# Values from unnormalised, host-transposed rows; forgetting heads first; their output projection moved into attention

## The chip, the core and the metric

The kernel runs on one core of one Trainium2 chip. The metric is the device time of one execution in microseconds (us), here the median of the runs of one kernel. The engines are named as in the profile: PE does matmuls (PEld is its weight load), DVE and ACT do elementwise work and read the banks that PE writes, POOL does slower elementwise work, and SP issues every DMA of this kernel, in the order of the program.

## What is computed

One layer on x of 1024 rows by 1024 columns, in float32. The part that the change touches, from the reference:

```python
h = rmsnorm(x, g_mix_pre)
fq, fk, fv, f_logit, cq, ck, cv = split(h @ w_in)          # 8 + 8 heads of 64
y_fox = forgetting_attention(fq, fk, fv, f_logit + b_fgt)  # causal; logits + c[t] - c[s]
                                                           # with c = cumsum(log_sigmoid(f_logit))
y_chk = chunked_relpos_attention(cq, ck, cv, rel_bias)     # own chunk of 64 + 8 before, relative bias
y = concat(rmsnorm(y_fox, g_fox_out), rmsnorm(y_chk, g_chk_out))
x = x + rmsnorm(y @ w_out, g_mix_post)
```

Cross-attention into 256 memory rows and a squared-ReLU MLP of width 4096 follow; of them the change touches only where the keys and values of the memory stand in the order of the work.

rmsnorm divides a row by the root of its mean square and multiplies it by a gain per column. A row's factor can therefore be applied after a product with weights, while the gain per column must go in ahead of it.

## The kernel before, in words

**Products.** Every product is in split form: each operand is a high part, rounded to the fast matmul type, plus a low part, the rest. mm3 (L191 to L195) issues three matmuls per product: high by high, low by high, high by low. A high part is an ACT copy out of a bank or a load (L187, L231, L404), its low part a DVE or POOL subtraction (L188, L232, L406 to L413).

**Banks.** The eight banks go in pairs under the tags mm, s, tr and pv. A pair under mm serves the projections: a third product waits until the evictions have emptied the first.

**Start-up (L1345 to L1404)**, written out by hand. Rows of x come in 128 at a time (L266); ACT squares and sums them (L208), POOL takes the root (L202, L203), DVE multiplies by root and gain (L272), PE transposes them 128 by 128 (L218), ACT and DVE split the result into hT, high and low (L231, L232). A gain row is spread over the partitions by two matmuls with ones (gpre, L1356). Behind each two blocks of rows the values of half of the heads are projected (values, L306 to L322): v1, the chunked heads' first half, and v0, the forgetting heads' first half with the eight gate columns (264 columns). The relative-bias rows are loaded, turned round and stored to DRAM between them (bias_rows, L280 to L286: rsrc, rrow, rd), and the first three weight blocks of the stock are loaded and two of them split.

**Attention phase (L1333)**. From here Flow (L58 to L135) writes out the order: streams of PE steps, each with a planned cost and a condition; work for DVE, ACT, POOL and DMA issue (V, S, G, D) is put into a planned time line and emitted in its order. The streams, by priority: value_steps (L686: pv, the products of probabilities and values), turn_steps (L649: transposes of probabilities), score_steps (L559), side_steps (L809: forget gates, then transposes of later values), rstd_steps(0) and, as filler, filler_steps (L1322): projections of q, k and from pair 4 also v for each pair of heads, then memory keys and values. Pairs go in ORDER (L325): chunked 0 and 1, forgetting 0 to 3, chunked 2 and 3. Stock (L346) loads weight blocks ahead into three buffers and splits them; Biases (L512) loads the row bias or the cumulative gate (cd) of each head; Outputs (L941) reloads the finished heads.

The forget gates (L469 to L493) are eight small transposes, a chain of ten DVE steps and three ACT steps with two table loads over 8 rows of 1024, which ends in a scan (L492) and a store to cd (L493).

**pv (L686 to L716).** A step covers two key blocks by two query blocks, of which one corner can be masked off ("dead"). The dead quarter of ph and pl, the split probabilities, is set to zero on POOL (L665, L666), and the step has four matmuls of 256 columns (L708, L709). When a unit is done, ACT copies 64 partitions of the bank (L715), DVE adds the other 64 (L716), and one DMA stores the result to od.

**Second phase.** filler: mix_steps(0) and mix_steps(1) (L1085), the two halves of the output projection, the second added to the first; then the memory queries and so on to the MLP.

Of the kernel before, what the change touches and what calls it, by code (L numbers as in the profile page):

```python
# [14 lines left out]
F32 = mybir.dt.float32  # L15
# [120 lines left out]
def build(ctx, tc, nc, out, t):  # L136
# [16 lines left out]
    def u4(name, shape, dt=F32R):  # L153

        return up.tile(list(shape), dt, tag="u4", bufs=30, name=name)
# [16 lines left out]
    wcount = [0]  # L172

    def load_w(src, shape, alloc=None, lo_on=None):
        n = wcount[0]
        wcount[0] += 1
        raw = wp.tile(shape, F32, tag="wraw", bufs=3, name=f"wraw{n}")
        nc.sync.dma_start(raw, src)
        return split_w(raw, shape, n, alloc, lo_on)

    def split_w(raw, shape, n, alloc=None, lo_on=None):
        if alloc is None:
            hi = wp.tile(shape, F32R, tag="whi", bufs=2, name=f"whi{n}")
            lo = wp.tile(shape, F32R, tag="wlo", bufs=2, name=f"wlo{n}")
        else:
            hi, lo = alloc(f"whi{n}", shape), alloc(f"wlo{n}", shape)
        nc.scalar.activation(hi, raw, AF.Copy)  # L187
        (lo_on or nc.gpsimd).tensor_sub(lo, raw, f(hi))  # L188
        return hi, lo

# [15 lines left out]
    def rms(x, scratch, name):  # L206
        ss = small.tile([P, 1], F32, tag="ss", bufs=8, name=f"ss_{name}")
        nc.scalar.activation(scratch, x, AF.Square, scale=1.0 / 32.0, accum_out=ss)  # L208
        return rstd_of(ss, f"rstd_{name}")

    def to_T(xa, xb, act, c0, name, tags=("tr", "tr")):

        trs = [mm_tile([P, 2, 2, P], f"tr_{name}_{k}", tags[k // 4]) for k in range(0, KC, 2)]

        def turn(k, q):
            xn = (xa, xb)[q]
            for j in range(2):
                nc.tensor.transpose(trs[k // 2][:, j, q, :], xn[:, (k + j) * P:(k + j + 1) * P], ident)  # L218

        ahead = tags[0] != tags[1]  # L220
        if ahead:
            for k in range(0, KC, 2):
                turn(k, 0)
        for k in range(0, KC, 2):
            if not ahead:
                turn(k, 0)
            turn(k, 1)
            src = trs[k // 2].rearrange("p a q b -> p a (q b)")
            i, o = k // act.per, k % act.per
            dh = act.h[i][:, o:o + 2, c0:c0 + 256]  # L230
            nc.scalar.activation(dh, src, AF.Copy)  # L231
            nc.vector.tensor_sub(act.l[i][:, o:o + 2, c0:c0 + 256], src, f(dh))  # L232


# [6 lines left out]
    ones = const.tile([1, P], F32, name="ones")  # L241
# [4 lines left out]
    od = [[dr.tile([P, HT], F32, name=f"od{k}_{h}") for h in range(2)] for k in range(KC)]  # L246
# [15 lines left out]
    hT = [Act(f"hT{h}") for h in range(2)]  # L262
    def load_x(b):
        tag = "sp" if b % 3 else "klo"
        xt = p1.tile([P, D], F32, tag=tag, bufs=5 if b % 3 else 4, name=f"x_{b}")
        nc.sync.dma_start(xt, t["x"][b * P:(b + 1) * P, :])  # L266
        return xt

    def norm_x(xt, b):
        junk = p1.tile([P, D], BF16, tag="ph", bufs=2, name=f"junk{b}")  # L270
        r = rms(xt, junk, f"x{b}")
        nc.vector.scalar_tensor_tensor(xt, xt, r, gpre, op0=ALU.mult, op1=ALU.mult)  # L272

# [14 lines left out]
    fcol = p1.tile([P, TB, 8], F32, tag="o2", bufs=2, name="fcol")  # L288

    def value_weights(g, raws=None, only=None):  # L290

        n = 264 if g == 0 else 256
        src = t["w_v0"] if g == 0 else t["w_v1"]
        raws = [] if raws is None else raws
        for i, (a, b) in enumerate(((0, 3), (3, 6), (6, 8)) if g == 0 else ((0, 4), (4, 8))):
            if only in (None, i):
                raw = wp.tile([P, b - a, n], F32, tag="wraw", bufs=3, name=f"wrawv{g}{a}")
                nc.sync.dma_start(raw, src[:, a:b, :])
                raws.append(raw)
        return raws  # L300

    def value_split(g, raw, i, lo_on=None):
        k = raw.shape[1]
        wh, wl = split_w(raw, list(raw.shape), f"v{g}{i}", None if g == 1 else u4, lo_on)
        return [(wh[:, j, :], wl[:, j, :]) for j in range(k)]

    def value_tiles(g):

        return [u4(f"vs{g}_{i}", (P, 2, 4, P)) for i in range(4)]

    def values(g, w, vs, kb):
        act, cs = hT[kb // 4], slice((kb % 4) * P, (kb % 4 + 1) * P)
        n = 264 if g == 0 else 256
        ps = mm_tile([P, n], f"v{g}_{kb}")
        for kc in range(KC):
            mm3(ps, act.hi(kc, cs), act.lo(kc, cs), *w[kc], kc == 0, kc == KC - 1)
        src = ps[:, 0:256].rearrange("p (h d) -> p h d", d=64)
        dh = vs[kb // 2][:, kb % 2, :, 0:64]
        nc.scalar.activation(dh, src, AF.Copy)
        if g == 0:  # L320
            nc.scalar.activation(fcol[:, kb, :], ps[:, 256:264], AF.Copy)
        nc.vector.tensor_sub(vs[kb // 2][:, kb % 2, :, 64:128], src, f(dh))  # L322


    ORDER = (("c", 0), ("c", 1), ("f", 0), ("f", 1), ("f", 2), ("f", 3), ("c", 2), ("c", 3))  # L325
# [3 lines left out]
            dict(s=2, tr=2, pv=2, mm=2, sp=1, p=2, klo=4, bias=2, raw=2, w=0, u4=6,  # L329
# [16 lines left out]
    class Stock:  # L346
# [3 lines left out]
        def __init__(self):  # L350
            self.blocks = []
            for n, (kind, pr) in enumerate(ORDER):
# [9 lines left out]
            self.blocks += [(("mk", nb), t["w_mk"][nb], [P, KC, P]) for nb in range(KC)]  # L362
            self.blocks += [(("mv", nh, kp), row_pair(t["w_mv"], kp, nh), [P, 2, HT])
                            for nh in range(2) for kp in range(4)]
            pair = [P, 2, HT]
            self.blocks += [(("wo", g, nh, i), row_pair(t["w_out"], 2 * g + i, nh), pair)
                            for g in range(2) for nh in range(2) for i in range(2)]
# [5 lines left out]
            self.home = {("wo", 0, 1, 0): "wq", ("wo", 0, 1, 1): "u4", ("wo", 1, 1, 0): "wq", ("wo", 1, 1, 1): "u4"}  # L373
# [95 lines left out]
    def forget_gates():  # L469

        z, e, l, u = [p1.tile([8, S], F32, tag="sp", bufs=5, name=f"f{n}") for n in "zelu"]
        parts = []
        for g in range(2):
            tr = mm_tile([8, 4, P], f"ftr{g}", "tr")
            for j in range(4):
                nc.tensor.transpose(tr[:, j, :], fcol[:, g * 4 + j, :], ident)
            parts.append(("V", 0.75, lambda g=g, tr=tr: nc.vector.tensor_scalar(
                z[:, g * HT:(g + 1) * HT], tr.rearrange("p a b -> p (a b)"), bfgt, None, op0=ALU.add)))
# [16 lines left out]
        def done(at):  # L495
            seen["gates"] = at
            for _ in range(4):
                free["sp"].give(at)

        for _ in range(2):  # L500
            free["tr"].take()
        flow.chain(flow.end, parts[:2], lambda at: [free["tr"].give(at) for _ in range(2)] and
                   flow.chain(at, parts[2:], done))


# [53 lines left out]
    def score_steps():  # L559
# [5 lines left out]
        for n, a in heads:  # L565
            kind, pr = ORDER[n]
            h = pr * 2 + a
            for g in groups(n):
                probs[n, a, g] = {}
                for q in (1, 0) if kind == "f" else (0, 1):  # L570
# [9 lines left out]
                    for j, (o, w) in enumerate(pieces):  # L580
# [21 lines left out]
                        if not last:  # L602
                            flow.put("V", flow.end, 0.15 + w / 950, reduce, free["s"].give)
                        else:
# [17 lines left out]
                            go = lambda at, w=w, reduce=reduce, after=after: flow.put("V", at, 0.15 + w / 950, reduce, after)  # L622
# [26 lines left out]
    def turn_steps():  # L649
        for n, a, g in units:  # L650
            for c, (kbs, slots, dead) in enumerate(key_steps(n, g)):
# [6 lines left out]
                whole = all_of(("t", n, a, g, c), 1 + len(dead))  # L658
# [3 lines left out]
                for m, (j, q) in enumerate(slots):  # L662
                    if m in dead:
                        def zero(ph=ph, pl=pl, m=m):
                            nc.gpsimd.memset(f(ph[:, m, :]), 0.0)  # L665
                            nc.gpsimd.memset(f(pl[:, m, :]), 0.0)  # L666
                        flow.put("G", flow.now, 0.45, zero, whole)
                    else:
                        sp, b0, i = probs[n, a, g][q]
                        k = kbs[j] - b0  # L670
                        nc.tensor.transpose(tr[:, m, :], sp[:, k * P:(k + 1) * P], ident)  # L671

                def split(at, ph=ph, pl=pl, tr=tr, live=live, whole=whole):
# [3 lines left out]
                    flow.put("V", at, 0.7, lambda: nc.vector.tensor_sub(pl[:, live, :], tr[:, live, :],  # L677
                                                                        f(ph[:, live, :])), done)

                flow.put("S", flow.end, 0.6, lambda ph=ph, tr=tr, live=live: nc.scalar.activation(  # L680
# [5 lines left out]
    def value_steps():  # L686
        landed = [all_of(("od", k), 32) for k in range(2)]
        for n, a, g in units:
            kind, pr = ORDER[n]
            h = pr * 2 + a  # L690
            own, oth = HALVES[a]
            kcol = pr if kind == "f" else 4 + pr
            steps = key_steps(n, g)
            for c, (kbs, slots, dead) in enumerate(steps):
                yield (0.48, lambda: there(("t", n, a, g, c), ("v", n, 0), ("v", n, 1))
                       and (c or free["pv"].ready()))
# [4 lines left out]
                for half in range(2):  # L701
                    kb = kbs[slots[2 * half][0]]
                    if n < 4:
                        v = vs[0 if kind == "f" else 1][kb // 2][:, kb % 2, (pr % 2) * 2 + a, :]
# [1358 lines left out]
```

## Time and profile before

| | us |
|---|---|
| median of 3 runs | 1495.92 (1494.37 to 1496.46) |
| the profiled execution: its time and its span | 1496.46, 1496.5 |
| PE busy, share of the span | 1475.1, 99% |
| DVE, ACT, POOL busy | 938.1, 789.8, 403.4 |
| first value matmul; first matmul of q | 11.96; 65.54 |
| end of the gates' scan | 91.55 |

How to read the rows below. A row of the table of windows is a stretch (start and end in us, its length), then for PE, PEld, DVE, ACT and POOL busy time and number of instructions, then the granted clock of PE (1.00 is full), the mean busy share of the DMA engines, and GB/s. A row of the timeline is start, length, engine, line, operation, output<-inputs, tile shapes and count, and in brackets the engine's idle time just before it with what ended that. A group row is line, engine, operation and shape, xcount, then busy us, mean ns of one, then idle time ahead of the group and what ended most of it. A DMA row has count, KB each, and us from issue to landing.

### The profile page before, as it was taken

The numbers are of one execution on the slowest core, as the hardware profiler recorded it, in microseconds if no ns is written. First come the engines' busy times: TensorE is split into PE (matmuls) and PEld (weight loads), VectorE is DVE, ScalarE is ACT, GpSimd is POOL, SyncE is SP. The second block draws the span as 40 slices with busy tenths as digits, with TensorE's granted clock in tenths as the row PEclk, the third lists the DMA queues.
The fourth block names the chain that finished last, engine by engine and source line by source line (L and its number), as shares of the span: only waits on it lengthen the run. The fifth ranks groups of instructions, "written<-read, shape, count | busy, mean of one in ns | idle before, by whom it ended". The sixth has DMA issues, their size and how long they took to land. (4 is left out here: it accounts for less than half of the span.)

```text
span 1496.5 us, 21618 instructions
## 1 busy us (share of the span) xinstructions
PE 1475.1 (99%) x7628; PEld 1254.1 (84%) x7628; DVE 938.1 (63%) x1617; ACT 789.8 (53%) x1405; POOL 403.4 (27%) x629
## 2 busy tenths in 40 slices
PE   8999999999999999999999999999999999999998
PEld 7989888888889888888888887888888888888886
DVE  6377677565576834884375577775555675646577
ACT  5367576575666835554354455555555553444442
POOL 4244355353354300521031423333333000000021
PEclk9999999999999999999999999999999999999999
DMA  4223312512225552461241355774445685436465
GB/s 170 90 74 89 84 44 88 152 55 65 73 66 149 173 177 85 137 213 59 85 169 57 112 183 186 265 246 147 150 150 176 234 340 202 140 120 215 173 252 197
DMA packets 82766, 218.58 MB, mean 146 GB/s; under 512 B 9801, under 2 KB 13905, under 8 KB 82658
## 3 DMA queue, kind: packets, MB, share of 16 engines
q1 hardware_dynamic: 82658, 217.20, 43.5%
q8 instruction: 60, 0.98, 0.3%
q14 instruction: 48, 0.39, 0.1%
HBM read 157.86 MB, written 50.91 MB: 140 GB/s over the span
## 5 line engine op out<-in xcount | busy, mean ns | idle before, releaser
L677 DVE TENSOR_TENSOR pl<-ptr,ph 128x512 fp32r<-128x512 f32 (+1 forms) x152 | 92.2, 616 | 39.7 <-ACT ph L680 33.7
L1789 ACT ACTIVATE whif<-ra 128x1024 fp32r<-128x1024 f32 x37 | 39.2, 1060 | 122.2 <-PE fy L194 62.6
L1791 DVE TENSOR_TENSOR wlof<-ra,whif 128x1024 fp32r<-128x1024 f32 x37 | 45.3, 1225 | 91.0 <-ACT whif L1789 91.0
L680 ACT ACTIVATE ph<-ptr 128x512 fp32r<-128x512 f32 (+1 forms) x152 | 79.3, 540 | 39.0 <-PE ptr L671 32.4
L1905 POOL TENSOR_SCALAR rf<-sf 128x1 f32<-128x1 f32 x8 | 8.2, 1026 | 326.4 <-ACT jf L1890 326.1
L709 PE MATMUL pv<-pl,vs 128*128 128x256 f32 x304 | 78.9, 283 | 2.6 <-DVE pl L677 2.6
L708 PE MATMUL pv<-ph,vs 128*128 128x256 f32 x304 | 79.8, 286 | 0.0
L194 PE MATMUL fx<-vlof,whif 128*128 128x512 f32 x168 | 65.4, 389 | 0.0
L193 PE MATMUL fx<-vhif,whif 128*128 128x512 f32 x168 | 65.4, 389 | 0.0
L195 PE MATMUL fx<-vhif,wlof 128*128 128x512 f32 x168 | 65.4, 389 | 0.0
L709 PEld LDWEIGHTS pv<-pl,vs 128*128 128x128 f32 x304 | 57.6, 189 | 7.4 <-DVE pl L677 2.2
L708 PEld LDWEIGHTS pv<-ph,vs 128*128 128x128 f32 x304 | 57.3, 188 | 4.0
L1679 POOL TENSOR_TENSOR sc<-wf,wf 128x512 f32<-128x512 f32 x14 | 21.3, 1524 | 142.3 <-DMA wf<-in_w_ff 95.4
L193 PE MATMUL k<-hT_hi,whik 128*128 128x512 f32 x128 | 52.7, 412 | 0.0
L193 PE MATMUL mq<-h2T_hi,whimq 128*128 128x512 f32 x128 | 51.6, 403 | 0.0
L193 PE MATMUL q<-hT_hi,whiq 128*128 128x512 f32 x128 | 50.9, 398 | 0.0
L193 PE MATMUL ym<-whimo,oT_hi 128*128 128x512 f32 x128 | 50.3, 394 | 0.1
L194 PE MATMUL yw<-wlowo,yT_hi 128*128 128x512 f32 x128 | 49.9, 390 | 0.3 <-DVE wlowo L410 0.3
L195 PE MATMUL k<-hT_hi,wlok 128*128 128x512 f32 x128 | 50.2, 392 | 0.0
L194 PE MATMUL mq<-h2T_lo,whimq 128*128 128x512 f32 x128 | 50.1, 391 | 0.1
L193 PE MATMUL yw<-whiwo,yT_hi 128*128 128x512 f32 x128 | 50.1, 392 | 0.0
L194 PE MATMUL k<-hT_lo,whik 128*128 128x512 f32 x128 | 50.1, 391 | 0.0
(596 smaller groups left out, 5029.2 us busy)
## 6 DMA issues: line engine op xcount, KB each, us to landing
ra<-gd SPq DMA_DIRECT2D x56, 512.0 KB, 3.9
wg<-in_w_ff SPq DMA_DIRECT2D x56, 512.0 KB, 6.0
wf<-in_w_ff SPq DMA_DIRECT2D x38, 512.0 KB, 4.0
gd<-s SPq DMA_DIRECT2D x48, 256.0 KB, 2.1
wrawmq<-in_w_mq SPq DMA_DIRECT2D x16, 512.0 KB, 3.8
wrawmo<-in_w_mo SPq DMA_DIRECT2D x16, 512.0 KB, 3.8
gd<-u SPq DMA_DIRECT2D x32, 256.0 KB, 2.1
gd<-g SPq DMA_DIRECT2D x25, 256.0 KB, 2.5
```

The lines of the kernel that those rows point to most:

```text
L193: nc.tensor.matmul(ps, lh, rh, start=start, stop=False, skip_group_check=more)
L194: nc.tensor.matmul(ps, lh, rl, start=False, stop=False, skip_group_check=more)
L195: nc.tensor.matmul(ps, ll, rh, start=False, stop=stop, skip_group_check=more)
L677: flow.put("V", at, 0.7, lambda: nc.vector.tensor_sub(pl[:, live, :], tr[:, live, :], f(ph[:, live, :])), done)
L680: flow.put("S", flow.end, 0.6, lambda ph=ph, tr=tr, live=live: nc.scalar.activation(ph[:, live, :], tr[:, live, :], AF.Copy), split)
L708: nc.tensor.matmul(pv, v, ph[:, hs, :], start=c == 0 and half == 0, stop=False)
L709: nc.tensor.matmul(pv, v, pl[:, hs, :], start=False, stop=c + 1 == len(steps) and half == 1)
L1679: eng.tensor_sub(sc[:, k1], r0[:, k0], r1[:, k0])
L1789: nc.scalar.activation(ah, ra, AF.Copy)
L1791: nc.vector.tensor_sub(al, ra, f(ah))
L1905: nc.gpsimd.tensor_scalar(r, ssf[b][:, 0:1], ssf[b][:, 1:2], EPS, op0=ALU.add, op1=ALU.add)
```

## The change

1. **Start-up.** x also comes transposed from the host (x_t, 128 columns of x by 512 rows per piece). Its pieces are multiplied by the gain and split (plain_split), with no root yet. The values are projected from them, and a row's root goes in when they leave the banks (values_out). Squares are still summed from rows of x; the root, on POOL, is set on four diagonals, and a matmul with ones spreads it over the partitions (spread). DVE then normalises x_t in place (norm) and it is split again into hT for q and k (norm_split). The 64 transposes of x and the gpre matmuls are gone. Values first projected are now both halves of the forgetting heads; the chunked values come with the pairs.
2. **Order.** Forgetting pairs 0 to 3, then chunked 0 to 3. The forget gates move from side_steps into the start-up, between norm and norm_split of the second half; both parts of bias_rows come after them. The first pair is projected as q and k of the first 512 columns, then q and k of the second.
3. **pv.** No zeros are written; a matmul on a half with a dead quarter has 128 columns instead of 256 (160 of 608).
4. **Leaving the pv bank.** One ACT copy of 128 by 256 and two stores, high and low half apart; Outputs loads both (16 more loads of 256 KB) and adds them, on POOL for the forgetting heads, on DVE for the chunked.
5. **mix_steps(0)** goes into attention's filler, after the memory keys and ahead of the memory values. Its result is stored to yd and loaded again for mix_steps(1) (Back).
6. **Planner.** Planned costs of three steps are lower (reduce, ph, pl), 34 buffers of the kind u4 instead of 30, the first two weight blocks are split into u4, and a smaller DMA scratch is declared.

```diff
-    ORDER = (("c", 0), ("c", 1), ("f", 0), ("f", 1), ("f", 2), ("f", 3), ("c", 2), ("c", 3))
+    ORDER = tuple((kind, pr) for kind in "fc" for pr in range(4))
...
-                            flow.put("V", flow.end, 0.15 + w / 950, reduce, free["s"].give)
+                            flow.put("V", flow.end, 0.1 + w / 1000, reduce, free["s"].give)
...
-                    if m in dead:
-                        def zero(ph=ph, pl=pl, m=m):
-                            nc.gpsimd.memset(f(ph[:, m, :]), 0.0)
-                            nc.gpsimd.memset(f(pl[:, m, :]), 0.0)
-                        flow.put("G", flow.now, 0.45, zero, whole)
-                    else:
+                    if m not in dead:
...
-                for half in range(2):
+                full = 1 if dead == [0] else 0
+                todo = [(full, ph), (1 - full, ph), (1 - full, pl), (full, pl)]
+                for m, (half, x) in enumerate(todo):
...
-                    hs = slice(2 * half, 2 * half + 2)
-                    nc.tensor.matmul(pv, v, ph[:, hs, :], start=c == 0 and half == 0, stop=False)
-                    nc.tensor.matmul(pv, v, pl[:, hs, :], start=False, stop=c + 1 == len(steps) and half == 1)
+                    qs_ = [k for k in (2 * half, 2 * half + 1) if k not in dead]
+                    k0, k1 = qs_[0], qs_[-1] + 1
+                    q0 = slots[k0][1]
+                    nc.tensor.matmul(pv[:, q0:q0 + k1 - k0, :], v, x[:, k0:k1, :], start=c == 0 and m == 0,
+                                     stop=c + 1 == len(steps) and m == 3, skip_group_check=True)
...
+                    nc.scalar.activation(box["t"][:, :, ::step], pv, AF.Copy)
...
+                    for m in range(2):
+                        flow.load(at, lambda m=m: nc.sync.dma_start(
+                            od[kcol][g // 2][m][a * 64:a * 64 + 64, (g % 2) * 256:(g % 2) * 256 + 256],
+                            box["t"][m * 64:m * 64 + 64].rearrange("p a b -> p (a b)")), done, 2.2)
...
     def second_filler():
-        yield from mix_steps(0)
         yield from mix_steps(1)
...
     def filler_steps(keep):
         for n in range(8):
             part = all_of(("qk", n), 12)
-            yield from project_steps("q", n, part)
-            if n > 3:
-                yield from project_steps("v", n, part)
-            yield from project_steps("k", n, part)
+            for ths in ((0,), (1,)) if n == 0 else ((0, 1),):
+                yield from project_steps("q", n, part, ths)
+                if n > 3:
+                    yield from project_steps("v", n, part)
+                yield from project_steps("k", n, part, ths)
         for _ in range(16):
             free["u4"].give(flow.end)
-        yield from memory_steps(keep)
+        yield from memory_key_steps(keep)
+        yield from mix_steps(0)
+        yield from memory_value_steps(keep)
...
+        def plain_split(th, kc):
+            x, g = xf[th][kc // 2][:, kc % 2, :], gp[:, kc:kc + 1]
+            h, l = hT[th].hi(kc), hT[th].lo(kc)
+            nc.scalar.activation(h, x, AF.Copy, scale=g)
+            nc.vector.scalar_tensor_tensor(l, x, g, f(h), op0=ALU.mult, op1=ALU.subtract)
...
+        V = value_banks(0, 1)
+        value_part(V, 1, w0, range(KC))
+        values_out(1, 0, W)
+        for b in range(4, 8):
+            square(b)
+            norm(0, b)
+        d = root(1)
+        for kc in range(KC):
+            norm_split(0, kc)
+        spread(1, d, "pv")
+        W = value_banks(1, 1)
+        value_part(W, 1, w1, range(4))
+        values_out(0, 1, V)
+        gates = forget_gates()
+        value_part(W, 1, w1, range(4, 8))
+        for _ in range(2):
+            gates.pop(0)()
+        stock.split_now(2)
+        for kc in range(KC):
+            norm(1, kc)
+            if kc > 1 and gates:
+                gates.pop(0)()
+        values_out(1, 1, W)
+        for kc in range(KC):
+            norm_split(1, kc)
+            if gates:
+                gates.pop(0)()
+        for call in gates:
+            call()
+        bias_rows(0)
+        bias_rows(1)
```

More of the change, by code (lines that the diff above doesn't have):

```diff
@@ L286, in bias_rows @@
         nc.sync.dma_start(rd, rrow)
[L288 to L322, printed above, removed]
-    ORDER = (("c", 0), ("c", 1), ("f", 0), ("f", 1), ("f", 2), ("f", 3), ("c", 2), ("c", 3))
+    fcol = p1.tile([P, TB, 8], F32, tag="fcol", name="fcol")
+    ORDER = tuple((kind, pr) for kind in "fc" for pr in range(4))
     HALVES = [(slice(a * 64, a * 64 + 64), slice(64 - a * 64, 128 - a * 64)) for a in range(2)]
@@ L493, in forget_gates @@
             ("D", 0.55, lambda: nc.sync.dma_start(cd, l))]
[L495 to L503, printed above, removed]
+        return [call for _, _, call in parts]
     bias, qs, kd, kl, vs2, probs, trs, pvs = {}, {}, {}, {}, {}, {}, {}, {}
@@ L804, in project_steps @@
                     flow.put("S", flow.end, 0.6, hi, then, 1)
-        free["w"].give(flow.end)
+        if 1 in ths:
+            stock.done((what, n))
     vt = {}
     def side_steps():
-        yield 0.87, lambda: flow.now > 2.5 and free["tr"].ready(2)
-        forget_gates()
         for n in range(4, 8):
@@ L949, in pump @@
                 th, g = self.left[0]
-                if not (there(("od", g), "scored") and free["u4"].ready(7) and (g == 0 or ("w", 1) in ys)):
+                if not (there(("od", g)) and ((th, g) == (0, 0) or there("keys")) and free["u4"].ready(14 if (th, g) == (0, 0) else 9)):
                     break
                 self.left.pop(0)
-                for _ in range(7):
+                for _ in range(9):
                     free["u4"].take()
@@ L1083, in close_row, with __init__, pump, y_half @@
         flow.put("G", at, 0.95, lambda: root(0, ss[:, 0:1], ss[:, 1:2]), wait, 1)
+    stored = [all_of(("yd", th), 8) for th in range(2)]
+    class Back:
+        def __init__(self):
+            self.left = [0, 1]
+        def pump(self):
+            while self.left and there(("yd", self.left[0])) and free["u4"].ready(6) and (
+                    there(("rs", 1, 1)) if self.left[0] else there("vm")):
+                th = self.left.pop(0)
+                y_tiles("w", th)
+                done = all_of(("yb", th), 4)
+                for b in range(4):
+                    flow.load(flow.now, lambda b=b, th=th: nc.sync.dma_start(ys["w", th][0][b], yd[th * 4 + b]), done)
+    def y_half(name):
+        return p1.tile([P, HT], F32R, tag="klo", bufs=4, name=name)
     def mix_steps(g):
@@ L1345, in build @@
     stock = Stock()
+    back = Back()
     with tc.manual_schedule():
[L1347 to L1357 removed]
@@ new lines, in build @@
+        w1 += wv_split(1, 1, nc.gpsimd)
+        square(3)
+        for b in range(4, 8):
+            load_row(b)
+        nc.sync.dma_start(bfgt, t["b_fgt"])
+        nc.sync.dma_start(gcol, t["g_heads"])
+        d = root(0)
+        stock.load(3)
+        W = value_banks(1, 0)
+        value_part(W, 0, w1, range(KC))
+        for kc in range(2):
+            plain_split(1, kc)
+        values_out(0, 0, V)
+        for kc in range(2, 4):
+            plain_split(1, kc)
+        spread(0, d, "s")
```

331 lines of the change are left out of this document (186 added, 145 removed).

## The prediction

> **What bounds the kernel now.** I read the page's busy shares first, then the table of windows, then the timeline of PE in the stretches where a window showed PE short of full.
>
> ```profile
> span 1496.5 us, 21618 instructions
> PE 1475.1 (99%) x7628; PEld 1254.1 (84%) x7628; DVE 938.1 (63%) x1617; ACT 789.8 (53%) x1405; POOL 403.4 (27%) x629
> ...
> 0.00:50.00 50.00, 43.83 (x324) 40.40 (x325) 28.50 (x40) 26.33 (x52) 18.40 (x25) 1.00 0.34 128
> 100.00:500.00 400.00, 399.15 (x2459) 352.79 (x2458) 267.79 (x767) 262.31 (x555) 186.02 (x391) 1.00 0.30 87
> 500.00:550.00 50.00, 47.06 (x258) 40.29 (x257) 34.43 (x60) 31.76 (x53) 7.40 (x15) 0.97 0.64 207
> 1200.00:1300.00 100.00, 100.00 (x442) 82.80 (x442) 66.10 (x60) 45.40 (x52) 0.00 (x0) 1.00 0.65 237
> ```
>
> PE is busy 99% of the span, so what counts is PE's work and its few gaps. The window of 1200 to 1300 gives the pace: 442 matmuls of 512 columns in 100 us, 0.226 us each. Attention (100 to 500) has under 1 us of idle PE in 400, so work that the change takes from DVE, ACT or POOL there buys nothing by itself. Gaps stand in two places only, the first 50 us and the turn from attention to the output projection (500 to 550). The profiled execution's span, 1496.46 us, is also its time (nothing lies around it); it is 0.5 us above the median of the three runs. I make the sum against 1496.5 and subtract that 0.5 at the end.
>
> **The change, part by part.**
>
> *The start up to the last value.*
>
> ```profile
> 4.82 1.06 ACT L208 ACTIVATE junk<-x 128x1024 bf16<-128x1024 f32 x1 [2.81 <-DMA x<-in_x]
> L231 ACT ACTIVATE hT_hi<-tr_x 128x512 fp32r<-128x512 f32 x16 | 8.3, 603 | 2.0 <-PE tr_x L218 2.0
> L986 DVE SCALAR_TENSOR_TENSOR yT_lo<-oin,gcol,yT_hi 128x512 fp32r<-128x512 f32 x16 | 11.5, 747 | 25.6 <-ACT yT_hi L985 25.6
> 8.31 3.89 PE L218 MATMUL tr_x<-ident,x 128*128 128x128 f32 x16 [2.30 <-DVE x L272]
> 11.96 0.36 PE L193 MATMUL v<-whiv,hT_hi 128*128 128x256 f32 x1
> 12.80 0.28 PE L194 MATMUL v<-wlov,hT_hi 128*128 128x256 f32 x1
> 17.95 0.29 PE L195 MATMUL v<-whiv,hT_lo 128*128 128x256 f32 x1
> 18.07 1.91 PE L218 MATMUL tr_x<-ident,x 128*128 128x128 f32 x16
> 65.54 0.39 PE L193 MATMUL q<-hT_hi,whiq 128*128 128x512 f32 x1
> 88.02 0.39 PE L195 MATMUL k<-hT_hi,wlok 128*128 128x512 f32 x1
> ```
>
> In before the first value matmul is at 11.96, after squares, root, norm, transposes and splits of the first rows; three later groups of 16 transposes (1.91 each) stand between value blocks. From 12.80 to 17.95 are 43 matmuls, 0.120 each. The 384 value matmuls (some with 264 columns, a hair longer) make 46.3 us, and q's first matmul is at 65.54.
>
> In after the first half piece of x_t (256 KB) with its weights (132 KB) is less than the 512 KB that ACT had at 4.82. Two ACT copies and a DVE low half (0.60 and 0.75, the second and third rows) bring the first value matmul to about 7.4. Until 11.9 before's PE ran at half pace: the 16 transposes at 8.31 take 3.89, those at 18.07 take 1.91. With the same until 11.9, after loses 2.2 there. Then 46.3 of values, two matmuls of ones by the diagonal (0.9 each), the eight gate transposes (0.9) and an estimated 1.7 of waits for evictions and for the two roots: 7.4 + 2.2 + 46.3 + 1.8 + 0.9 + 1.7 = 60.3; laid out engine by engine I get 60.9, and take that for the start of q0. In before q0 begins at 65.54 and still has the gate transposes (1.0) in its way. So **the start gains 5.6 us**, if the next step lets it.
>
> *The gates, now before the bias rows and the stock.*
>
> ```profile
> 68.29 1.03 PE L476 MATMUL ftr<-ident,fcol 128*8 128x128 f32 x8
> 68.93 1.40 DVE L477 TENSOR_SCALAR fz<-ftr,bfgt 8x512 f32<-8x512 f32 x2 [2.27 <-PE ftr L476]
> 73.35 1.06 ACT L483 ACTIVATE fe<-fl 8x1024 f32<-8x1024 f32 x1
> 79.87 1.28 ACT L487 ACT_TABLE_LOAD   x1
> 81.17 1.06 ACT L487 ACTIVATE fu<-fl 8x1024 f32<-8x1024 f32 x1
> 82.26 1.33 DVE L488 TENSOR_TENSOR fe<-fe,fu 8x1024 f32<-8x1024 f32 x1 [2.07 <-ACT fu L487]
> 89.27 2.28 DVE L492 TENSOR_TENSOR_SCAN fl<-fe,fu 8x1024 f32<-8x1024 f32 x1
> 91.57 0.29 SPq L493 DMA_DIRECT2D cd<-fl  x1
> 50.76 0.27 DVE L283 TENSOR_SCALAR rrow<-rsrc 8x256 f32<-8x256 f32 x1
> 51.06 0.42 DVE L285 COPY rrow<-rrow 8x511 f32<-8x511 f32 x1
> 51.51 0.29 SPq L286 DMA_DIRECT2D rd<-rrow  x1
> wrawk<-in_w_qk SPq DMA_DIRECT2D x8, 512.0 KB, 3.6
> L404 ACT ACTIVATE whik<-wrawk 128x1024 fp32r<-128x1024 f32 x8 | 8.5, 1059 | 0.1
> L788 ACT ACTIVATE qs<-q 64x512 fp32r<-64x512 f32 x32 | 18.9, 591 | 25.6 <-PE q L195 23.9 <-DVE qs L789 1.5
> L789 DVE SCALAR_TENSOR_TENSOR qs<-q,qs 64x512 fp32r<-64x512 f32 x32 | 22.0, 689 | 20.4 <-ACT qs L788 19.8
> ```
>
> In before the bias rows went out at 51.5, long ahead of the gates, and cd at 91.57 ran beside the q and k projections. In after SP issues in this order: three weight blocks, cd, the load of rsrc, the store rd, and only then the weights of k for pair 1. SP takes its queue in order: cd waits for the scan, rd waits on DVE's rrow, which waits for rsrc. Behind it on ACT, the high half of those k weights stands ahead of the first q eviction, because the code's planner gave it that place. And q's second half needs a bank: two banks hold q0 and k0 of the first half until DVE's low halves of q have emptied the first. So PE's next matmul after k0 hangs on the whole chain scan, cd, rsrc, rrow, rd, load, ACT split, eviction.
>
> The times: from the end of the gate transposes (69.3) to the end of the scan (91.55) before took 22.2 us. In after the transposes end near 55.3, with 16 norm and low-half steps of DVE (about 0.7 each) laid between the gates' steps; placed one after the other by these durations the scan ends at 78.6, which is 23.3. The bare chain (no other work between, table loads counted) would take 16, so not before 71.3; with all DVE work in series 28.7, so 84. I take 78.6, which is nearest to the row. Then: issue of cd and rsrc 0.5, rsrc lands 1.6 (the first small load was used 1.55 after its issue), rrow 0.8 (50.76 to 51.48), issue of rd and of the load 0.5, landing 3.6, split 1.1, two evictions 1.2, low half 0.7: 10.0, and q's second half starts at 88.6.
>
> q0 and k0 of the first half (48 matmuls, 10.9) end at 71.8. **PE waits 16.8 us** (9.5 to 22 by the ends). The second halves take 10.9 and end at 99.5.
>
> ```profile
> 517.00:521.00 4.00, 4.00 (x13) 3.18 (x12) 3.90 (x7) 3.82 (x9) 0.00 (x0) 0.57 0.08 20
> 515.40 0.39 PE L709 MATMUL pv<-pl,vs 128*128 128x256 f32 x1 [1.63 <-DVE pl L677]
> ```
>
> After much shorter waits at 505 to 517 the granted clock was 0.57 of full over 4 us, which cost 1.7. I add that once: 101.2. In before k0 ends at 88.2 (88.02 and one pace). So the start as a whole, the 5.6 included, is **13 us later**; by the ends of the chain from +6 to +18. Nothing covers the wait: scores need cd and k0, and no other projection has a bank.
>
> *The turn to the second phase.* In 500 to 550 PE is idle 2.9 (50 less 47.06) and 1.7 goes to the clock; rows like the one at 515.40, 0.39 long where its kind takes 0.28, hide a little more. The cause is in that row: the last units wait for DVE's pl, and PE has nothing else to do. In after the first output projection (192 matmuls, 43.5 us) and the memory values are filler at that place. I take **−5**; the ends are 0 and −6. Its 16 stores and 8 reloads go where the DMA share is 0.30 (100 to 500); 16 more half loads of 256 KB cost no time of PE.
>
> *Narrower pv matmuls.*
>
> ```profile
> L709 PE MATMUL pv<-pl,vs 128*128 128x256 f32 x304 | 78.9, 283 | 2.6 <-DVE pl L677 2.6
> L666 POOL MEMSET pl<- 128x128 f32 x80 | 16.4, 206 | 0.0
> 525.47 0.95 PE L1004 MATMUL ssh<-o,sq 128*128 128x1 f32 x8
> 2.27 3.75 PE L1356 MATMUL gpre<-grow,ones 1*128 1x512 f32 x4 [2.27 <-DMA grow<-in_g_mix_pre]
> ```
>
> Of the 608 pv matmuls 160 go from 256 to 128 columns. No matmul of this split type below 256 columns is in the trace. With one moving column the ssh row still takes 0.95 for 8, and the 16 transposes of 128 columns take 1.91; as the last of a group lasts some 0.28 from its start (the rows at 12.80 on), that is (1.91 − 0.28)/15 = 0.109 each. So the weight change looks like a floor near 0.11: 160 × (0.120 − 0.1105) = **−1.5**. Paid by column it would be 160 × 0.060 = −9.6. At the plain float pace, gpre's 3.75 for 1024 columns at half clock, 128 columns take 0.234: 160 × 0.114 = +18. I take the floor, the nearest in shape. The 160 memsets (33 us) leave POOL, which waits in attention already: 0.
>
> The Trainium skill (TensorE: Matmul & The Clock Gate, LDWEIGHTS) gives a weight load as the columns over 1.2, so 107 ns for 128: by it the narrowing is −2.1, against −1.5 by the row. Its section Back-to-back issue gap gives 81 ns for 128 columns, which would make it −6.2; the 0.109 of the transposes of 128 columns doesn't bear that out.
>
> *Eviction of the outputs.*
>
> ```profile
> L716 DVE TENSOR_TENSOR ot<-pv,o 64x256 f32<-64x256 f32 x64 | 26.7, 417 | 21.6 <-ACT o L715 19.9 <-DMA od<-ot 0.8
> ```
>
> DVE loses 64 adds (26.7 us); ACT's copy has the same columns on twice the partitions; 16 adds come back on reload, half on POOL, and SP gets 64 more stores. All of it lies in a stretch in which PE idles under 1 us of 400, so 0. The lower planned costs and the order of heads may move waits there: ±3.
>
> Sum: 1496.5 + 13 − 5 − 1.5 = 1503.0, less 0.5 for the median: **1502.5 us**.
>
> **The rivals.** *No stall.* The gate chain runs near its bare 16 us, because DVE's other steps fit under ACT's table loads. The change turns into a gain where the start costs less than the 6.5 that the rest brings: with a stall under about 10 us, so a scan before about 72. With the scan at 71.3 the time is 1495; were the k load not behind the chain at all, the second halves would end at 82.7, 5.5 before the old time: 1496.5 − 5.5 − 5 − 1.5 − 0.5 = 1484. For it: before's chain had other work between, too. Against: 11 us of norm steps are written between the gates in program order.
>
> *Narrow matmuls at the plain float pace.* The pv of 128 columns cost +18 and not −1.5: 1502.5 + 19.5 = 1522. For it: the scores are kept at 256 columns or more in the code. Against: no row shows it.
>
> *The turn isn't cured.* The last scores end the wait as before, or the tighter planned costs bring new waits, while the filler has been used up early: 0 for −5, 1507.5.
>
> **How the numbers follow.** Main forecast 0.54, with its own range 1496 to 1509 (chain and turn). No stall 0.15, narrow pace 0.19, turn not cured 0.12. A measurement here tells about 0.2%, 3 us, from no change: 1493 to 1499 is "same". Faster: of the no-stall case 0.12. Same: its rest 0.03 and 0.06 of the main case, 0.09. Slower 0.79. The range leaves out the no-stall times and the highest of the narrow case: 1493 to 1524.
>
> **What would show it.** First value matmul near 7.4 and q0 near 61; then PE idle for about 17 us from 72, released through DVE's qs, with ACT waiting for the load of k's weights and SP's rd just before it, and a clock below full after. In pv, 128-column matmuls a pace of 0.11 apart (0.23 would be the second rival). At the end of attention no 1.6 us waits on pl. Wrong I would be if the k load of pair 1 is issued before 70, or if attention itself shows tens of us of PE idle.

## The result and the profile after

The changed kernel takes 1517.16 us (median of 4 runs, 1515.42 to 1519.01), the kernel before 1495.54 on the same chip: ratio 1.0146, 95% interval 1.0132 to 1.0160. The forecast was 6.6 us slower (1502.5 against the 1495.92 known then); it is 21.6 slower. The first lines of the page, and then rows of the table of windows, of the kernel after:

```profile
span 1514.7 us, 21395 instructions
PE 1468.5 (97%) x7564; PEld 1248.1 (82%) x7564; DVE 929.5 (61%) x1585; ACT 795.5 (53%) x1424; POOL 390.7 (26%) x472
```
```profile
0.00:50.00 50.00, 38.81 (x290) 37.83 (x290) 26.36 (x45) 32.89 (x60) 12.63 (x18) 1.00 0.67 243
50.00:100.00 50.00, 29.28 (x163) 25.20 (x164) 32.04 (x45) 20.18 (x34) 19.36 (x11) 0.80 0.14 46
500.00:550.00 50.00, 47.71 (x342) 43.99 (x341) 38.92 (x104) 38.01 (x83) 28.02 (x27) 1.00 0.55 171
1200.00:1300.00 100.00, 99.17 (x438) 81.81 (x437) 67.42 (x64) 45.52 (x51) 0.00 (x0) 1.00 0.74 278
```

PE is busy for 6.6 us less, 97% of the span and not 99%. One window tells nearly all: from 50 to 100 PE is busy 29 of 50 us, at a mean clock of 0.80, where before had 50 of 50 at 1.00. The row of before:

```profile
50.00:100.00 50.00, 50.00 (x292) 43.88 (x290) 25.93 (x46) 20.76 (x37) 12.90 (x17) 1.00 0.36 110
```

Nothing of that size stands anywhere else.

First a correction of the base. In every run of both kernels that lists a span, the time is 1.8 us over it (after: 1516.47 and 1514.7). So the profiled execution of before, with its span of 1496.5, took about 1498.3 by that measure: it was not the run of 1496.46, and stands 2.7 over the median of its kernel, where the prediction took 0.5. After's profiled execution lies 0.7 under its own median. So the two traces are 18.2 apart, the medians 21.6.

Where the 18.2 come from, by stages: the second halves of the first q and k end at 109.0 (the 96th projection matmul starts at 108.79) and not at 88.2, **+20.8**. For the rest I summed, over PE's timeline, what lies between the starts of neighbouring matmuls beyond the usual pace of their width (0.2265 for 512 columns, 0.120 for 256, 0.109 for 128): attention from 100 to 500 has 10.1 us of such small waits where before had 7.0, **+3.1**; the stretch from 500 to 600 has 4.3 instead of 6.2, **−1.9**; the 160 narrow pv matmuls, counted at 0.109 for 0.120, give **−1.8**; the second phase, which the change barely touches, gives −2.

The lines that carry the +20.8, from the timelines of PE, SP, ACT and DVE of the kernel after:

```profile
8.14 0.59 PE L174 MATMUL v<-whiv,hT_hi 128*128 128x264 f32 x1 [8.14 <-ACT hT_hi L1355]
52.01 2.08 PE L1377 MATMUL rt<-diag,ones 128*128 128x512 f32 x2 [5.06 <-POOL diag L1372]
96.63 0.77 PE L174 MATMUL q<-hT_hi,whiq 128*128 128x512 f32 x1 [18.71 <-DVE qs L695]
```
```profile
20.31 20.95 SPq L1318 DMA_DIRECT2D x<-in_x  x5
...
85.92 0.30 SPq L401 DMA_DIRECT2D cd<-fl  x1
86.32 0.29 SPq L223 DMA_DIRECT2D rsrc<-in_rel_rev  x1
88.83 0.27 SPq L229 DMA_DIRECT2D rd<-rrow  x1
89.28 0.35 SPq L299 DMA_DIRECT2D wrawk<-in_w_qk  x1
```
```profile
44.66 1.06 ACT L1362 ACTIVATE junk<-x 128x1024 bf16<-128x1024 f32 x1 [1.68 <-DMA x<-in_x]
...
92.92 1.06 ACT L312 ACTIVATE whik<-wrawk 128x1024 fp32r<-128x1024 f32 x1 [12.75 <-DMA wrawk<-in_w_qk]
93.88 1.18 ACT L694 ACTIVATE qs<-q 64x512 fp32r<-64x512 f32 x2
```
```profile
60.86 1.40 DVE L385 TENSOR_SCALAR fz<-ftr,bfgt 8x512 f32<-8x512 f32 x2 [3.53 <-PE ftr L384]
83.63 2.27 DVE L400 TENSOR_TENSOR_SCAN fl<-fe,fu 8x1024 f32<-8x1024 f32 x1
88.08 0.27 DVE L226 TENSOR_SCALAR rrow<-rsrc 8x256 f32<-8x256 f32 x1
95.09 1.39 DVE L695 SCALAR_TENSOR_TENSOR qs<-q,qs 64x512 fp32r<-64x512 f32 x2 [6.29 <-ACT qs L694]
```

The fences are of PE, SP, ACT and DVE, in this order; read them from the last row up. PE's long wait ends with DVE's low half of q at 95.09, that waited for ACT's high half (93.88), which stood behind the split of the k weights (92.92, after 12.75 us of idle ACT), whose load SP issued at 89.28, behind rd, rsrc and cd; and cd waited for the scan, which ended at 85.90. That is the forecast chain, link for link. Ahead of it stands a wait that was not forecast: the second spread matmul at 52.01 waited 5.06 for the diagonals. ACT's last square came at 44.66, because its row had only then landed: SP took 20.95 us for five loads of x rows, each of which needs the buffer of an earlier row's square (with the squares earlier, in the second experiment, the same five take 8.37).

### The profile page after: what moved, and what is told of

Read it like the earlier page. It is cut to its first block, busy times and chain, and to the rows that moved or that the text cites. A ratio compares the mean times of both kernels' runs of the same rounds, so it can differ in the third digit from the quotient of the medians.

```text
span 1514.7 us, 21395 instructions
## 1 busy us (share of the span) xinstructions
PE 1468.5 (97%) x7564; PEld 1248.1 (82%) x7564; DVE 929.5 (61%) x1585; ACT 795.5 (53%) x1424; POOL 390.7 (26%) x472
## 5 line engine op out<-in xcount | busy, mean ns | idle before, releaser
L174 PE MATMUL q<-hT_hi,whiq 128*128 128x512 f32 x128 | 51.8, 405 | 18.7 <-DVE qs L695 18.7
L605 PE MATMUL pv<-pl,vs 128*128 128x256 f32 (+1 forms) x304 | 64.6, 294 | 0.7 <-DVE pl L571 0.7
L605 PEld LDWEIGHTS pv<-ph,vs 128*128 128x128 f32 x304 | 53.0, 189 | 8.3 <-ACT ph L574 0.5
L605 PE MATMUL pv<-ph,vs 128*128 128x256 f32 (+1 forms) x304 | 57.4, 270 | 0.1
L175 PE MATMUL q<-hT_lo,whiq 128*128 128x512 f32 x128 | 50.6, 395 | 0.0
L176 PE MATMUL q<-hT_hi,wloq 128*128 128x512 f32 x128 | 50.5, 395 | 0.0
```

The costliest lines, as they stand in the source:

```text
L174: nc.tensor.matmul(ps, lh, rh, start=start, stop=False, skip_group_check=more)
L175: nc.tensor.matmul(ps, lh, rl, start=False, stop=False, skip_group_check=more)
L176: nc.tensor.matmul(ps, ll, rh, start=False, stop=stop, skip_group_check=more)
L605: nc.tensor.matmul(pv[:, q0:q0 + k1 - k0, :], v, x[:, k0:k1, :], start=c == 0 and m == 0, stop=c + 1 == len(steps) and m == 3, skip_group_ ...
```

## The experiments

All times stand beside runs of the kernel before on the same chip (its medians were 1495.9 to 1496.2). Differences from after are taken between the ratios, 1% being 15 us; by the intervals such a difference is uncertain by about 3 us, and one between two runs with intervals of 0.09% either way by about 2.

| run | us | ratio to before, interval |
|---|---|---|
| after | 1517.2 | 1.0146 (1.0132 to 1.0160) |
| bias rows and k load early | 1512.4 | 1.0107 (1.0091 to 1.0124) |
| squares early | 1513.0 | 1.0109 (1.0094 to 1.0124) |
| both | 1506.6 | 1.0063 (1.0050 to 1.0077) |
| gates by the planner alone | 1506.5 | 1.0068 (1.0056 to 1.0081) |
| both, and gates by the planner | 1494.2 | 0.9982 (0.9973 to 0.9991) |
| the same, old planned costs | 1493.6 | 0.9986 (0.9977 to 0.9995) |
| the same, zeros back | 1496.8 | 1.0009 (1.0000 to 1.0018) |
| the same, mix 0 after attention | 1520.9 | 1.0167 (1.0153 to 1.0181) |
| old costs, last squares later | 1493.1 | 0.9986 (0.9977 to 0.9995) |
| and the gates 4 us later | 1490.4 | 0.9968 (0.9955 to 0.9980) |

**The order on SP.** Bias rows into the bias buffers right behind the second root, and the k load of pair 1 ahead of cd:

```diff
         d = root(1)
+        bias_rows(0)
         for kc in range(KC):
             norm_split(0, kc)
+        bias_rows(1)
...
         stock.split_now(2)
+        stock.load(1)
...
-        bias_rows(0)
-        bias_rows(1)
```

> After, with the two bias-row steps moved ahead of the gates (their tiles in two other buffers) and the load of pair 1's k weights issued before the store of cd. Theory A (the wait of 18.7 us at 78 to 96.6 hangs first on SP's order: scan, cd, rsrc, rd, load, split, eviction; behind that DVE's queue is the next to be late): q's second half starts when DVE's low halves of hT and of q are through, near 89.6 and not 96.6, so about 7 us less than after, 1510. Rival B (SP's order alone is the cause): the bank is free near 83.8, 13 us less, 1504. Rival C (DVE's gates and norm steps alone set it): nothing, 1517.

It is 5.8 us less than after by the ratios (4.8 by the medians). The wait before q's second half is 10.7 and not 18.7. The timelines of PE and DVE in this run show it, and what is late next:

```profile
90.31 0.76 PE L174 MATMUL q<-hT_hi,whiq 128*128 128x512 f32 x1 [10.70 <-DVE qs L695]
```
```profile
84.24 2.27 DVE L400 TENSOR_TENSOR_SCAN fl<-fe,fu 8x1024 f32<-8x1024 f32 x1
86.44 2.32 DVE L1390 TENSOR_TENSOR hT_lo<-xf,hT_hi 128x512 fp32r<-128x512 f32 x2
88.77 1.39 DVE L695 SCALAR_TENSOR_TENSOR qs<-q,qs 64x512 fp32r<-64x512 f32 x2
```

ACT had evicted q by 82.8, but DVE's queue holds scan and the last low halves of hT ahead of the low half of q. So theory A holds and B falls, as C does: SP's order accounts for 8 us of the wait; that DVE's order of gates and norm steps makes the remaining 10.7 is what the run with the gates moved, below, shows.

**The late squares.**

```diff
-        for b in range(4, 8):
+        for b in range(4, 6):
             load_row(b)
+        for b in range(4, 6):
+            square(b)
+        for b in range(6, 8):
+            load_row(b)
...
         values_out(0, 0, V)
+        for b in range(6, 8):
+            square(b)
...
         for b in range(4, 8):
-            square(b)
             norm(0, b)
```

> After, with the squares of rows 4 and 5 straight behind those of the first four and of rows 6 and 7 before the second pieces are split, so that the loads of the last rows aren't held on SP until 41. Theory A: the wait of 5.1 us for the second diagonal goes, the gate transposes come 5 to 6 us earlier, and as everything behind them hangs on the gates' chain the whole is 5 to 6 us shorter, 1511.5. Rival D (the wait at 78 to 96.6 is set by loads or by DVE work that doesn't depend on the gates' start): that wait grows by as much, and the time stays within 1 us of 1517.

> Both edits of the two runs before. Theory A: they stand one behind the other on the same chain, so they add: 12 to 13 us less than after, 1504.5. If one covers the other (rival D): no more than the larger of the two, 1510.

Alone it is 5.5 us less, with the first edit 12.4 less (by the medians 4.1 and 10.6): within the uncertainty they add, as theory A says, and rival D falls. In the run with the squares alone q begins at 61.12 (after: 66.85, forecast: 60.9), the wait before its second half is as long as in after (the start of that half moves from 96.63 to 90.62). What comes earlier at the head of the chain comes earlier at its end.

**The gates in the planner's hands.** The gates' steps behind the first two go through flow.chain, among the evictions, and no longer stand between norm and norm_split:

```diff
         for kc in range(KC):
             norm(1, kc)
-            if kc > 1 and gates:
-                gates.pop(0)()
...
+        flow.chain(4.0, gates, gates_done)
```

> The run before, and the gates' steps behind the first two given to the planner (from planned time 4 on, so among the evictions of q and k) and not written between norm and norm_split; their tiles in two bias and two klo buffers. Theory A: the low halves of hT are done near 70, q's bank is free near 73, PE waits 2 us and not 18.7, and q and k of the first two pairs cover the gates up to 106: 23 us less than after, 1494. Rival E (forgetting heads first need cd so early that the wait only moves ahead of the first score): the gates end some 20 us later than q0 and k0 need, and 8 to 15 us come back as a wait on the bias load: 1504 or more.

> After, with only the gates' steps given to the planner (squares, bias rows and the k load stay where after has them; cd is then issued behind the k load by itself). Theory A: the long wait before q's second half goes but for 2 to 3 us, the 5 to 6 us of the late squares stay: 1500. Rival (the k load and the bias rows must move as well): a wait of 8 us or more stays there, 1506 or more.

With the two edits before it the time is 1494.2, 0.18% (0.09 to 0.27) below the kernel before: 24.5 less than after, so all of its loss and a little more. PE's wait is 1.9, by its timeline:

```profile
73.99 0.47 PE L174 MATMUL q<-hT_hi,whiq 128*128 128x512 f32 x1 [1.91 <-DVE qs L696]
```

Rival E falls: the bias load of the first head is issued at 90.61, the first reduce runs at 98.02, and no wait of over 0.9 stands there, since q and k of the second pair fill the time. Alone, without the two edits, the gates' move brings 11.7: my 1500 was wrong, and the time is the rival's, with a wait of 6.6 where it said 8 or more. The timelines of PE and SP in that run say why:

```profile
85.49 0.77 PE L174 MATMUL q<-hT_hi,whiq 128*128 128x512 f32 x1 [6.56 <-DVE qs L696]
```
```profile
77.71 0.29 SPq L229 DMA_DIRECT2D rd<-rrow  x1
78.17 0.36 SPq L299 DMA_DIRECT2D wrawk<-in_w_qk  x1
```

cd no longer blocks SP, but rd does: its rrow stands on DVE behind the low halves of hT, the k load behind it goes out at 78.17, ACT's q eviction follows it, and those 6.6 us of wait are left. The wait for the second root stands there too (4.9).

**The other parts of the change**, each taken back from the run with the gates moved:

> The run e4_gates_by_planner with the planned costs of reduce, ph and pl as they were before. Theory F (the lower planned costs put PE's steps ahead of what DVE and ACT can do, which is the 3 to 4 us by which attention's small waits between 100 and 500 grew): those waits fall from about 11 us to before's 7, and the time by 3 to 4, to 1490.5. Rival G (the small waits come with the new order of heads and the tail of the planner's order, not with the costs): within 1 us of 1494.

The small waits from 100 to 500 fall from 11.2 to 8.9 (the wait for a reduce before a score from 0.49 to 0.17), those from 500 to 600 grow from 3.1 to 4.1. The time is 0.5 shorter by the medians and 0.6 longer by the ratios, each with an interval of 1.3: no difference is shown, and theory F's 3 to 4 us are not there.

> The run e4_gates_by_planner with the zeros written on POOL again and all 608 pv matmuls 256 columns wide. Theory H (the weight change sets the pace of the narrow matmuls, 0.107 to 0.12, and POOL's 33 us of zeros lie beside it): 160 times 0.012, 2 us longer, 1496. Rival (paid by column): 9.6 longer, 1504. Rival (POOL's zeros hold up turns): over 4 longer, with pv waiting on POOL.

2.6 longer by the medians, 4.0 by the ratios, uncertain by 2: near theory H's 2 and far from the 9.6 of a price by the column. The run takes back the zeros with the width and can't part them, but no pv waits on POOL in it, so the memsets look off the path.

```diff
     def filler_steps(keep):
...
         seen["keys"] = flow.end
-        yield from mix_steps(0)
         yield from memory_value_steps(keep)
...
     def second_filler():
+        yield from mix_steps(0)
         yield from mix_steps(1)
```

> The run e4_gates_by_planner with the output projection of the forgetting heads back behind attention, as before: no yd, the weight blocks in the old order. Theory J (that projection was the filler that shortened the turn): the turn's loss goes back from about 3 to 6 us, 1497 in all. Rival K (memory keys and values were filler enough once forgetting heads go first, and the stores and reloads bought nothing): within 1 us of 1494.

26.8 longer by the medians: neither theory. (The edit also takes back the stores of yd, the order of the weight blocks, and the place of the root of the chunked outputs' first half.) PE's timeline has two waits that neither named:

```profile
555.85 1.84 PE L922 MATMUL ssh<-o,sq 128*128 128x1 f32 x8 [13.61 <-DVE sq L879]
565.83 1.84 PE L922 MATMUL ssh<-o,sq 128*128 128x1 f32 x8 [6.65 <-DVE sq L879]
```

Both are the sums of squares of the chunked outputs, which come last in the new order and are reloaded in twice as many pieces. Those reloads are issued between 530.5 and 551.3, while the DMA engines are at 1.03 of their time in the window from 530 to 545; the planner counts 3.0 us for one, and those whose landing the profile has took 4.7 to 8.8. So the sums come onto PE too early, ahead of nearly all matmuls of the projection that could have covered the reloads. The two waits make 20.3 of the 26.8, and from 545 to 572 the granted clock is 0.50 besides. What the projection is worth for the turn, this run does not tell.

**Two more edits in the start-up**, on the run with the old planned costs: the squares of rows 6 and 7 behind the last pieces of x_t, and the chain of the gates from planned time 8.

> The same with the gates from planned time 4 on, as in e5: only the edit of the squares. The wait at 37 to 39 goes, that at 75 stays: 1 to 1.5 us less than e5, 1492.3. If rows 6 and 7 then come late for the second diagonal, nothing is gained: 1493.6 or more.

> The run e5_old_planned_costs with two more edits in the start-up: the squares of rows 6 and 7 behind the last pieces of x_t (in e4 and e5 PE waited 1.6 to 1.9 us for the first spread factor, which stood behind them on ACT), and the planner's gates from planned time 8 and not 4 on, so that DVE's low halves of q stand ahead of the first gates' steps. If both waits hang on these orders, the 1.4 over the matmul's own time at 37 to 39 goes and of the 2.3 at 75 all but a few tenths: 3 us less than e5, 1490.5. If the later gates only push the first score back (cd some 2 us later, first score waiting on the bias load), the gain is 1 to 1.5, 1492.5.

The squares alone: 1493.1, within the interval of the run before; the wait at 38 is gone, but the one before q's second half grows from 2.3 to 3.0 start to start. With the gates later as well, q's second half starts one pace behind k (70.57 after 70.34) and behind the first matmul no wait over 0.4 is left ahead of 76; the time is 1490.4, 0.32% (0.20 to 0.45) below the kernel before, and the fastest of all.

## Why the prediction was wrong in size

*The start up to the last value: wrong by 6.0* (q0 at 66.85, forecast 60.9). This is the step that failed: the sum had 1.7 for evictions "and for the two roots". The first value matmul came at 8.14 and not 7.4 (7.7 to 9.8 in these kernels), which cost little; the second root alone cost 5.06 of idle PE, and a clock of 0.68 for 5 us behind it, which is another 1.6: 6.7 in the place of 1.7. First that window, then POOL's timeline, with the first root and the second, then DVE's beside the second:

```profile
52.00:57.00 5.00, 4.99 (x24) 3.96 (x25) 1.59 (x4) 2.87 (x10) 0.00 (x0) 0.68 0.00 0
```
```profile
28.12 0.24 POOL L1368 TENSOR_SCALAR rall<-ss 128x4 f32<-128x4 f32 x1 [1.82 <-ACT junk L1362]
28.44 1.05 POOL L1369 TENSOR_TENSOR rall<-rall,mhalf 128x4 f32<-128x4 f32 x1
29.59 1.79 POOL L1372 TENSOR_SCALAR diag<-ident,rall 128x128 f32<-128x128 f32 x4
...
45.90 0.41 POOL L1368 TENSOR_SCALAR rall<-ss 128x4 f32<-128x4 f32 x1 [14.51 <-ACT junk L1362]
46.39 1.56 POOL L1369 TENSOR_TENSOR rall<-rall,mhalf 128x4 f32<-128x4 f32 x1
48.05 3.91 POOL L1372 TENSOR_SCALAR diag<-ident,rall 128x128 f32<-128x128 f32 x4
```
```profile
46.36 5.09 DVE L1390 TENSOR_TENSOR hT_lo<-xf,hT_hi 128x512 fp32r<-128x512 f32 x8
```

I had not followed SP's queue for the x rows: three buffers for eight rows tie each load to a square on ACT, and ACT has the squares of rows 4 to 7 only from 39.74 on, behind its splits and evictions. But the queue is not all of the 5.06. The last square waited 1.68 for its row; and the second root took 6.1 us on POOL (45.90 to 51.96) where the first, by the same steps, took 3.3 (28.12 to 31.39): beside the low halves of hT on DVE the diagonals took 0.98 to 1.32 each, and the last, behind them, 0.37. The run with the squares early brings q to 61.12, 0.2 from the forecast. It makes the whole root earlier (it ends at 39.70), so it shows that the late root cost this, and not how much of it each part did.

*A reading.* The prediction says that before's gaps stand in two places only. Its table of windows has more: PE idles 1.5 us from 750 to 800 and 2.3 from 900 to 1000. This lies in the second phase, to which the sum gave nothing and which came out 2 us shorter.

*The gates and the wait: right in mechanism and links, short in size.* q's second half started at 96.63, forecast 88.6. Of the 8.0, 6.0 came in with the late gate transposes (by start plus length they end at 61.3 and not 55.3), 1.3 in the gates (from there to the end of the scan 24.6 and not 23.3), 0.7 between scan and q (10.7 and not 10.0). The wait itself was 18.7 and not 16.8. The clock after it was 0.62 in the 3.9 us that follow, close to before's 0.57, from which the sum took it (windows of the kernel after):

```profile
78.00:96.60 18.60, 0.00 (x0) 0.00 (x1) 12.07 (x16) 5.48 (x9) 9.85 (x4) 0.62 0.26 88
96.60:100.50 3.90, 3.87 (x11) 3.16 (x12) 1.29 (x2) 0.00 (x0) 0.00 (x0) 0.62 0.58 190
```

The experiments agree with the chain and correct one thing in it: I said that without the k load behind SP the second halves would start with no wait. With the load out of the way 10.7 us remained, because DVE's queue had the same gates ahead of the same low halves. Two queues held the same thing up, and only taking the gates out of both freed it.

*The turn: right sign, too large.* Forecast −5, measured −1.9 (6.2 to 4.3 over the paces). The waits on pl fell from four, 2.6 in all, to one of 0.69, and scores waiting for a bank came (timeline of PE, kernel after):

```profile
504.83 0.38 PE L492 MATMUL sc6g<-kd,qs 128*128 128x256 f32 x1 [0.87 <-DVE mnc6g L496]
546.74 0.50 PE L605 MATMUL pv<-pl,vs 128*128 128x128 f32 x2 [0.69 <-DVE pl L571]
```

The result lies within the ends that I gave (0 to −6). Why it is not more stays open: the run that would have told has its own waits, on the reloads.

*The narrow matmuls: right in the sum, wrong in the picture.* The forecast had them 0.11 apart, each with a floor of its own; they are not, and the sum came out because something else, by its fit the weight loads, has that size (last section).

*Evictions and planned costs: 0 with ±3*; measured +3.1 in attention, of which the old costs take back about 2 of small waits but no time that can be told. Its cause stays open.

*The base*: the two profiled executions lie 2.7 over and 0.7 under their medians, 3.4 together. In all: 6.5 forecast by the terms, +7.8 for the start, +3.1 for the turn, +3.1 in attention, −0.3 for pv, −2 in the second phase, +3.4 for the base: 21.6, as measured. This adds up by its making, since the terms are read from the two traces.

*The rivals.* No stall: didn't come, and the bare gate chain was nowhere near. The narrow pace: ruled out by the paces. The turn not cured: partly, by 3 of its 5 us. The range's upper end, 1524, was set by the narrow pace; the time lies inside it, but for another reason.

## What to carry to other kernels

When a step moves ahead of others, write down for each in-order queue it uses (here SP, ACT and DVE) what now stands behind it, and follow the first bank or buffer that PE needs through all of them: the gates blocked q through SP and through DVE, and removing either alone left 7 to 11 us. Loads into fewer buffers than there are pieces belong to the same list, since each waits for the reader of an earlier piece and holds up every load behind it. And work that was written by hand between two other chains can be better off in the planner that knows what waits for what: the same change with a handful of edits of order goes from 1.5% slower to 0.3% faster.

## What the runs showed of the hardware

A narrow matmul does not cost its floor by itself. In pv's steps (256, 128, 128, 256 columns) the paces in the kernel after (medians of 80 steps) are 0.117, 0.060, 0.112 and, to the matmul behind the step, 0.170; in before 0.117 to 0.120. So a 128-column matmul lets the next one start after 0.060, half of a 256-column one, but two matmuls on the time is given back: 0.46 for the step against 0.474. The weight loads fit this: inside these steps they start 0.109 to 0.118 apart (medians), and four at about 0.115 make 0.46. This agrees to within 10% with the Trainium skill (TensorE: Matmul & The Clock Gate, LDWEIGHTS), which gives a weight load as the columns over 1.2, so 107 ns for 128, and not with the 81 ns of its section Back-to-back issue gap, as far as these weights of float32 type go.

POOL and DVE lengthen some of each other's steps. Besides the second root above, rows of the timelines of the kernel after: the same POOL step first with DVE idle, then with DVE at work, and in the second fence a DVE step that took 0.68 in before:

```profile
57.85 2.55 POOL L321 TENSOR_TENSOR wloq<-wrawq,whiq 128x512 fp32r<-128x512 f32 x2 [5.89 <-ACT whiq L312]
60.35 5.05 POOL L321 TENSOR_TENSOR wlok<-wrawk,whik 128x512 fp32r<-128x512 f32 x2
```
```profile
64.17 1.77 DVE L389 TENSOR_SCALAR fl<-fz 8x1024 f32<-8x1024 f32 x1
```

2.55 became 5.05, and 0.68 became 1.77. In the run with the bias rows early the two don't meet: POOL's step runs from 60.83 to 63.37 and takes 2.54, the DVE step starts at 65.87 and takes 0.67, and the gates take 23.6 and not 24.6. So the meeting fits about 1.1 of the 1.3 us by which they were longer than forecast; that run moves other steps as well, so this is not shown by itself.
